# Second feed-forward product: weight sums by other formulas, one ahead of each of the third to sixth products

## The chip, the core and the metric

The kernel runs on one core of a Trainium2 chip. A core has a matrix engine (PE, with its weight loads listed apart as PEld), a vector engine (DVE), a scalar engine (ACT), a general engine (POOL) and a queue that issues transfers (SP). Each engine works through its own list of instructions; semaphores tie the lists together. PE sums its products in PSUM, a small memory of eight banks that DVE and ACT read out. The metric is device time in microseconds (us); before the change the median of three timed runs is 2292.98 us (2292.85 to 2294.41).

## The reference, cut to what matters

One transformer-like layer on 512 tokens of width 2048. Its last step, and the only one that the change touches, is the second product of the feed-forward part:

```python
D_MODEL = 2048
SEQ = 512
D_FF = -(-(8 * D_MODEL) // (3 * 256)) * 256      # 5632
...
h = rms_norm(x, norm2_g[layer]) * (1.0 + sc2) + sh2
gate, up = jnp.split(h @ w_ffn_in[layer], 2, axis=-1)
x = x + g2 * ((jax.nn.silu(gate) * up) @ w_ffn_out[layer])
```

All is float32. The second product is (512 x 5632) times (5632 x 2048).

## The kernel before, in words

**Seven products in place of eight.** The second product is done as a 2 x 2 block product by Winograd's form of Strassen's scheme: seven block products on sums and differences of the blocks. The weights' four blocks are called y[0] to y[3] in the code (y[0] top left, y[1] top right, y[2] bottom left, y[3] bottom right, each 128 partitions x n x 512 numbers). The sums of the other factor (the activations) are made ahead and lie in DRAM, from where `load_op` fetches them; the sums of the weights are made on DVE in this stage.

**Units.** The 44 row tiles of the inner dimension, paired by the scheme into 22, are cut into six chunks of 3, 3, 4, 4, 4 and 4 (`CHUNKS`), and the columns into two halves i. A pass over one chunk and one half is a unit; there are twelve, numbered u = 0 to 11. In a unit the seven products run in the order 2, 1, 7, 6, 4, 5, 3 (`ORDER`); the place of a product in that order is q = 0 to 6. Below, p2 is the product numbered 2, and so on.

**A product** (`multiply`, line 1195) goes through its chunk in pieces of two row tiles, here called halves h1 and h2 (in chunks of 3 the second half is one tile). Each half is first split into a high and a low part: ACT casts it to the matrix engine's reduced float (line 231), DVE subtracts the result from the original (line 232). PE then multiplies high by high, high by low and low by high, all into one bank: 12 matmuls of 128 x 512 per full half and pair of banks (j = 0 and 1), 24 for a product of four tiles. The halves' split tiles are named wfo in the profile (opsB for every fourth, which lies in spare room). In the engines' order below, wfo_2_0 is place q = 2 (p7), first half.

**The weight sums** of a unit are four, each on both halves. p2 and p1 take y[2] and y[0] as they are loaded and p3 takes y[3]; p7, p6, p4 and p5 take sums. Line 1268 makes y[0] = y[1] - y[0] ahead of p7; line 1202 makes y[1] = y[3] - y[1] for p7, t2 = y[3] - y[0] for p6 and y[2] = y[2] - t2 for p4. p5 takes the y[0] made ahead of p7. t2 is the tile T in the profile (from unit 1 on).

**Banks.** p1, p6, p5 and p3 write the two banks foA (foA_18351 is j = 0, foA_18352 is j = 1); p7 and p4 write foC; p2 writes foB. p1 starts foA anew, so its first matmul on a bank waits until p3's result of the unit before has been read out of it. That is the add `V.tensor_add(dst(0, j, 1), A[j], dst(0, j, 1))` at line 1289 (1285 after the change), on DVE, one for each bank. p1's own result is copied out by ACT (line 1222, in the first chunk line 1217).

**What sets the order.** The code is not run in the order written: a scheduler turns it into one fixed list for each engine, by dependencies and priorities. Splits and weight sums stand in `tc.high_priority(offset=AHEAD)` (300), ACT's copies out of foA and foC in twice that; the adds at line 1289 and 1282 have no raised priority.

**Loads.** y[0] and y[2] of the next unit are asked for at a unit's start, y[1] after p7 and y[3] after p3 (`load_y`, line 1048); y[1] and y[3] have one buffer each (yraw) that is loaded again when its last reader is done.

Of the kernel before, what the change touches and what calls it, by code (L numbers as in the profile page):

```python
# [26 lines left out]
CHUNKS = (3, 3, 4, 4, 4, 4)  # L27
ORDER = (2, 1, 7, 6, 4, 5, 3)
AHEAD = 300
# [100 lines left out]
def trunk(ctx, tc, a):  # L130
    nc = tc.nc
    V, S, G = nc.vector, nc.scalar, nc.gpsimd
# [91 lines left out]
    def split(r, shape, name):  # L224
        count[0] += 1
        if spare and count[0] % 4 == 0:
            hi, lo = spare[0](shape, name)
        else:
            hi, lo = ring_pair(shape, name)
        with tc.high_priority(offset=AHEAD):  # L230
            S.copy(hi, r)  # L231
            V.tensor_sub(lo, r, hi.bitcast(F32))  # L232
        return hi, lo
# [697 lines left out]
    for i, hs in enumerate(halves):  # L931
# [15 lines left out]
        y = rb[:, hs]  # L947
# [47 lines left out]
    for j in range(HALF):  # L995
        V.tensor_sub(block(0, 0, j), block(0, 1, j), block(0, 0, j))
        t2 = ft.tile([P, HT], F32, tag="t", name=f"t2_{j}")
# [35 lines left out]
    def place(n):  # L1033
        n %= 11
        return places[0][:, n] if n < 4 else places[1][:, n - 4] if n < 7 else places[2][:, n - 7]

    def load_op(c, q):
        if c < len(CHUNKS):
            nc.sync.dma_start(place(7 * c + q)[:, 0:CHUNKS[c]].bitcast(F32),
                              opd[c][:, ORDER[q] - 1].rearrange("p n (h t) -> p n h t", h=2))  # L1040

    def load_y(u, b):
        if u == len(units):
            return
        c, i = units[u]
        n = CHUNKS[c]
        t = raw_tile([P, n, T], f"wfo{u}_{b}") if b % 2 == 0 else yraw[u > 0][:, b // 2, 0:n]
        nc.sync.dma_start(t, a["w_fo"][i, b][:, starts[c]:starts[c] + n])
        blocks[u][b] = t
# [145 lines left out]
    def multiply(out, c, q, raw, first, u, sums):  # L1195
        n = CHUNKS[c]
        x = place(7 * c + q)
        for k0 in range(0, n, 2):
            w = min(2, n - k0)
            with tc.high_priority(offset=AHEAD):  # L1200
                for d, e, g in sums:
                    V.tensor_sub(*(t[:, k0:k0 + w] for t in (d, e, g)))
            whi, wlo = split(raw[:, k0:k0 + w], [P, w, T], f"wfo{u}_{q}_{k0}")
            for j in range(2):
                js = slice(j * P, j * P + P)
                for kk in range(w):
                    k = k0 + kk
                    flags = dict(stop=False, skip_group_check=True)
                    PE.matmul(out[j], x[:, k, 0, js], whi[:, kk], start=first and k == 0, **flags)
                    PE.matmul(out[j], x[:, k, 0, js], wlo[:, kk], start=False, **flags)  # L1210
                    flags["stop"] = k == n - 1
                    PE.matmul(out[j], x[:, k, 1, js], whi[:, kk], start=False, **flags)

    def onto(dst, src, first):
        if first:
            with tc.high_priority(offset=2 * AHEAD):
                S.copy(dst, src)
            return
        t = cond[:, taps[0] % 4 * T:taps[0] % 4 * T + T]
        taps[0] += 1  # L1220
        with tc.high_priority(offset=2 * AHEAD):
            S.copy(t, src)
        V.tensor_add(dst, dst, t)
# [14 lines left out]
    def some_out(n):  # L1238
        for _ in range(min(n, len(outs))):
            emit_out(*outs.pop(0))  # L1240

    for u, (c, i) in enumerate(units):
        def dst(th, j, dh):
            return O[:, 2 * th + j, dh * 1024 + i * T:dh * 1024 + i * T + T]

        def ready(th, dh):
            if c == last_c:
                outs.extend((8 * dh + 4 * i + m, th) for m in range(4))

        first, final = c == 0, c == last_c  # L1250
        if final and i == 0:
            for g in range(4):
                nc.sync.dma_start(place(7 * c + 7 + g).bitcast(F32).rearrange("p n h t -> p n (h t)"), x1d[:, 4 * g:4 * g + 4])
        if u == 2:
            nc.sync.dma_start(ident2, a["cst"][:, 0])
        y = blocks[u]
        t2 = (T2 if u else yraw[0][:, 2])[:, 0:CHUNKS[c]]
        load_y(u + 1, 2)
        load_y(u + 1, 0)
        for q, p in enumerate(ORDER):  # L1260
            out = {2: B[i], 7: C, 4: C}.get(p, A)
            raw = {2: y[2], 1: y[0], 7: y[1], 6: t2, 4: y[2], 5: y[0], 3: y[3]}[p]
            sums = {7: [(y[1], y[3], y[1])], 6: [(t2, y[3], y[0])], 4: [(y[2], y[2], t2)]}.get(p, ())
            if p == 7:
                with tc.high_priority(offset=AHEAD):
                    for k0 in range(0, CHUNKS[c], 2):
                        ks = slice(k0, min(k0 + 2, CHUNKS[c]))
                        V.tensor_sub(y[0][:, ks], y[1][:, ks], y[0][:, ks])
            multiply(out, c, q, raw, p in (1, 7) or p == 2 and first, u, sums)
            if final:  # L1270
                some_out(3)
            for j in range(2):
                if p == 1:
                    onto(dst(0, j, 0), A[j], first)
                    if final:
                        V.tensor_add(dst(0, j, 0), B[i][j], dst(0, j, 0))
                elif p == 7:
                    onto(dst(1, j, 1), C[j], first)
                elif p == 6:
                    onto(dst(1, j, 0), A[j], first)  # L1280
                elif p == 4:
                    V.tensor_add(dst(1, j, 0), C[j], dst(1, j, 0))
                elif p == 5:
                    onto(dst(1, j, 1), A[j], False)
                elif p == 3:
                    if first:
                        S.copy(dst(0, j, 1), A[j])
                    else:
                        V.tensor_add(dst(0, j, 1), A[j], dst(0, j, 1))
            if p == 1:  # L1290
                ready(0, 0)
                if final:
                    slots += [t[:, h * HT:h * HT + HT] for t in B[i] for h in range(2)]
            elif p in (4, 5, 3):
                ready(*{4: (1, 0), 5: (1, 1), 3: (0, 1)}[p])
            if p == 7:
                load_y(u + 1, 1)
            if p == 3:
                load_y(u + 1, 3)
            if u == 0 and q == 6:  # L1300
                places.append(hp.tile([P, 4, 4, 2, HT], F32R, tag="hhi", name="opsC"))
            if q < 4 and i == (c == 0):
                load_op(c + 1, q)
            if i == 1 and 1 <= q < 4:
                load_op(c + 1, q + 3)
# [60 lines left out]
```

## Time and profile before

| what | value |
|---|---|
| timed runs, median (lowest to highest) | 2292.98 us (2292.85 to 2294.41) |
| the profiled execution's own time | 2288.73 us |
| its span, first to last instruction | 2286.7 us |
| mean granted PE clock | 0.995 |
| PE busy over the span | 2228.2 us (97%) |
| DVE busy over the span | 1915.4 us (84%) |
| ACT busy over the span | 1156.0 us (51%) |
| second product, first and last matmul on foA, foB, foC start at | 1836.8 and 2278 us |

The profile is of one execution; its own time is 4.25 us under the median of the timed runs. In the rows of the timeline, the first number is the start in us from the span's start, the second the length; then engine, line, operation, output<-inputs, shape and count (xN merges N like instructions that follow each other). A bracket at the end says how long the engine was idle just before and which engine and line ended that.

### The profile page before, as it was taken

Reading aid. Unit: us, or ns where it says so; the run is one execution under the profiler, and the core shown is the slowest. Engines: PE = TensorE matmul, PEld = TensorE weight load, DVE = VectorE, ACT = ScalarE, POOL = GpSimd, SP = SyncE. Lnnn points to the kernel's source line nnn. Section 1 sums busy time; section 2 is a strip of 40 time slices with the busy share of each in tenths; the row PEclk is TensorE's granted clock in tenths of the full one; section 3 lists DMA queues with packets and bytes.
Section 4 is the critical chain, followed back from the end, with each engine's and each line's share of the span. In section 5 each row is a group of like instructions: output and inputs, shape, how many; then the busy total and the mean of one; then the engine's idle time right before and its main releaser. Section 6 shows DMA issues by size and latency. Waiting matters only on the chain.

```text
span 2286.7 us, 35537 instructions
## 1 busy us (share of the span) xinstructions
PE 2228.2 (97%) x14171; PEld 2025.8 (89%) x14171; DVE 1915.4 (84%) x2566; ACT 1156.0 (51%) x2015; POOL 10.0 (0%) x25
## 2 busy tenths in 40 slices
PE   7999899999999999999999999999999999999999
PEld 6899899878888878899999999999999977778787
DVE  8887779899887865599999888888888878888888
ACT  4326666566655522565454545455555445544443
POOL 0000000000000000000000000000000000000000
PEclk9999999999999999999999999999999999999999
DMA  9886546853332386346555644444444586666452
GB/s 369 314 326 220 174 145 228 303 188 111 112 110 74 111 310 228 97 143 226 185 208 198 225 149 169 150 153 166 132 171 143 178 310 225 238 221 221 151 199 75
DMA packets 114977, 437.68 MB, mean 191 GB/s; under 512 B 9822, under 2 KB 58236, under 8 KB 76796
## 3 DMA queue, kind: packets, MB, share of 16 engines
q1 hardware_dynamic: 114812, 435.42, 53.1%
q8 instruction: 111, 1.82, 0.3%
q14 instruction: 54, 0.44, 0.1%
HBM read 386.61 MB, written 48.77 MB: 190 GB/s over the span
## 4 chain that ended last, share of the span: by engine, by line
PE 64%; DVE 20%; DMA 7%; issue 5%; ACT 3%; SPq 0%; DVEq 0%; ACTq 0%
PE ffA L93 10%; PE foA L93 9%; PE wo L93 7%; PE sbp L93 7%; PE ffC L93 5%; PE foC L93 4%; PE st L93 4%; PE hgf L93 3%; PE hgg L93 3%; PE hgq L93 3%; DVE ff L232 3%; DMA opd<-fhi 2%; PE ffB L93 2%; PE ff L93 2%; DVE ada L179 1%
## 5 line engine op out<-in xcount | busy, mean ns | idle before, releaser
L93 PE MATMUL sbp<-wsb,hhi 128*128 128x384 f32 x1024 | 269.8, 343 | 3.1 <-DVE wsb L232 1.7
L179 DVE SCALAR_TENSOR_TENSOR ada<-ada,cond 128x2048 f32<-128x2048 f32 x95 | 217.0, 2289 | 48.1 <-DMA ada<-in_w_ada 47.9
L93 PEld LDWEIGHTS sbp<-wsb,hhi 128*128 128x128 f32 x1024 | 185.2, 190 | 7.9 <-issue 3.3
L93 PE MATMUL sbp<-wsb,hlo 128*128 128x384 f32 x512 | 172.9, 338 | 0.0
L93 PE MATMUL wo<-ohi,wo 128*128 128x512 f32 x480 | 150.2, 392 | 4.1 <-ACT wo L231 1.6
L232 DVE TENSOR_TENSOR wfo<-wfo,wfo 128x1024 fp32r<-128x1024 f32 (+1 forms) x72 | 83.3, 1164 | 39.7 <-ACT wfo L231 39.3
L93 PEld LDWEIGHTS wo<-ohi,wo 128*128 128x128 f32 x480 | 89.7, 188 | 24.3 <-ACT wo L231 2.9
L93 PE MATMUL ffA<-opD,ff 128*128 128x256 f32 x768 | 99.0, 286 | 4.0 <-ACT u L1027 4.0
L231 ACT CAST wfo<-wfo 128x1024 fp32r<-128x1024 f32 (+1 forms) x72 | 72.2, 1007 | 60.1 <-PE foA L93 56.9
L93 PE MATMUL ffC<-opC,ff 128*128 128x256 f32 x768 | 94.7, 279 | 5.8 <-ACT c L1027 5.8
L93 PEld LDWEIGHTS ffA<-opD,ff 128*128 128x128 f32 x768 | 95.6, 194 | 4.5 <-ACT u L1027 4.5
L1101 ACT CAST fhi<-forms 128x512 fp32r<-128x512 f32 (+1 forms) x63 | 43.7, 693 | 109.3 <-DMA opd<-fhi 76.2
L93 PEld LDWEIGHTS sbp<-wsb,hlo 128*128 128x128 f32 x512 | 97.0, 190 | 0.8 <-issue 0.5
L93 PEld LDWEIGHTS ffC<-opC,ff 128*128 128x128 f32 x768 | 90.8, 188 | 7.2 <-ACT c L1027 7.2
L93 PE MATMUL ffA<-opB,ff 128*128 128x256 f32 x768 | 93.3, 277 | 1.7 <-ACT ff L231 1.0
L93 PE MATMUL wo<-olo,wo 128*128 128x512 f32 x240 | 93.5, 390 | 0.1
L93 PE MATMUL ffB<-opA,ff 128*128 128x256 f32 x768 | 92.7, 276 | 0.0
L93 PEld LDWEIGHTS ffA<-opB,ff 128*128 128x128 f32 x768 | 90.1, 188 | 2.2 <-ACT ff L231 1.2
L93 PE MATMUL ffA<-opA,ff 128*128 128x256 f32 x744 | 89.9, 276 | 0.8 <-DVE ff L232 0.8
L93 PE MATMUL ffA<-opC,ff 128*128 128x256 f32 x744 | 90.1, 277 | 0.0
L93 PEld LDWEIGHTS ffB<-opA,ff 128*128 128x128 f32 x768 | 89.8, 188 | 0.0
L93 PE MATMUL ffC<-opB,ff 128*128 128x256 f32 x744 | 89.7, 276 | 0.0
(1008 smaller groups left out, 5955.5 us busy)
## 6 DMA issues: line engine op xcount, KB each, us to landing
ada<-in_w_ada SPq DMA_DIRECT2D x95, 1024.0 KB, 5.2
wfo<-in_w_fo SPq DMA_DIRECT2D x16, 1024.0 KB, 5.7
yraw<-in_w_fo SPq DMA_DIRECT2D x16, 1024.0 KB, 4.9
fix<-in_w_fix SPq DMA_DIRECT2D x14, 1024.0 KB, 5.5
opd<-forms SPq DMA_DIRECT2D x44, 256.0 KB, 4.7
opd<-fhi SPq DMA_DIRECT2D x42, 256.0 KB, 4.4
opsC<-opd SPq DMA_DIRECT2D x10, 1024.0 KB, 4.8
opsA<-opd SPq DMA_DIRECT2D x9, 1024.0 KB, 7.0
```

What stands on the lines that cost most here:

```text
L93: self.engine.matmul(out, lhsT, rhs, **kw)
L179: V.scalar_tensor_tensor(w, w, 1.0, row, op0=ALU.mult, op1=ALU.mult, accum_out=col)
L231: S.copy(hi, r)
L232: V.tensor_sub(lo, r, hi.bitcast(F32))
L1101: S.copy(hi, R[:, q])
```

## The change

t2 is the same quantity by another formula: y[3] - (y[1] - y[0]) becomes y[0] + (y[3] - y[1]), which uses the y[1] already made for p7. So the difference y[1] - y[0] isn't wanted before p6 any more. It is only p5's operand, and it is now made ahead of p5 as y[3] - t2. Each of p7, p6, p4 and p5 so has one sum made ahead of it; before, p7 had two and p5 none. Since y[1] is now read by p6's sum, its next load is asked for after p6 in place of p7. The numbers of sums, splits, matmuls and transfers stay the same.

```diff
             with tc.high_priority(offset=AHEAD):
-                for d, e, g in sums:
-                    V.tensor_sub(*(t[:, k0:k0 + w] for t in (d, e, g)))
+                for combine, *tiles in sums:
+                    combine(*(t[:, k0:k0 + w] for t in tiles))
...
-            sums = {7: [(y[1], y[3], y[1])], 6: [(t2, y[3], y[0])], 4: [(y[2], y[2], t2)]}.get(p, ())
-            if p == 7:
-                with tc.high_priority(offset=AHEAD):
-                    for k0 in range(0, CHUNKS[c], 2):
-                        ks = slice(k0, min(k0 + 2, CHUNKS[c]))
-                        V.tensor_sub(y[0][:, ks], y[1][:, ks], y[0][:, ks])
+            sums = {7: [(V.tensor_sub, y[1], y[3], y[1])], 6: [(V.tensor_add, t2, y[0], y[1])],
+                    4: [(V.tensor_sub, y[2], y[2], t2)], 5: [(V.tensor_sub, y[0], y[3], t2)]}.get(p, ())
             multiply(out, c, q, raw, p in (1, 7) or p == 2 and first, u, sums)
...
-            if p == 7:
+            if p == 6:
                 load_y(u + 1, 1)
```

The scheduler's lists change with it, at three places that the prediction speaks of.

**DVE in unit 8**, from the split of p1's first half on. L232 is a split's subtraction, L1202 and L1268 are the sums, L1289 and L1285 the adds that read p3's result of the unit before out of foA. First before, then after:

```order
L232 TENSOR_TENSOR wfo_1_0_20166<-wfo_0_19890,wfo_1_0_20166 128x1024
L1289 TENSOR_TENSOR O<-foA_18351,O 128x512
L1268 TENSOR_TENSOR wfo_0_19890<-yraw,wfo_0_19890 128x1024
L232 TENSOR_TENSOR wfo_1_2_20181<-wfo_0_19890,wfo_1_2_20181 128x1024
L1202 TENSOR_TENSOR yraw<-yraw 128x1024
L1268 TENSOR_TENSOR wfo_0_19890<-yraw,wfo_0_19890 128x1024
L1202 TENSOR_TENSOR T_18348<-yraw,wfo_0_19890 128x1024
L232 TENSOR_TENSOR wfo_2_0_20204<-yraw,wfo_2_0_20204 128x1024
L1202 TENSOR_TENSOR yraw<-yraw 128x1024
L1202 TENSOR_TENSOR T_18348<-yraw,wfo_0_19890 128x1024
```

```order
L1202 TENSOR_TENSOR yraw<-yraw 128x1024 x2
L232 TENSOR_TENSOR wfo_1_2_20181<-wfo_0_19890,wfo_1_2_20181 128x1024
L1202 TENSOR_TENSOR T_18348<-wfo_0_19890,yraw 128x1024
L232 TENSOR_TENSOR wfo_2_0_20202<-yraw,wfo_2_0_20202 128x1024
L1202 TENSOR_TENSOR T_18348<-wfo_0_19890,yraw 128x1024
L1202 TENSOR_TENSOR wfo_2_19888<-wfo_2_19888,T_18348 128x1024
L232 TENSOR_TENSOR opsB<-yraw,opsB 128x1024
L1202 TENSOR_TENSOR wfo_2_19888<-wfo_2_19888,T_18348 128x1024
L232 TENSOR_TENSOR wfo_3_0_20238<-T_18348,wfo_3_0_20238 128x1024
L1202 TENSOR_TENSOR wfo_0_19890<-yraw,T_18348 128x1024 x2
L1285 TENSOR_TENSOR O<-foA_18351,O 128x512
```

Before, the add for the first bank stood right behind the split of p1's first half, and the one for the second bank (not shown) after all eight sums. Now both stand after all eight sums, the first one thirteen instructions behind that split, the second two rows further. Units 6 and 10 read the same. In units 5, 7 and 9 the new list reads, behind the split of p2's second half: sum y[1] h1, split p1 h1, sum y[1] h2, sum t2 h1, split p1 h2, sum t2 h2, split p7 h1, sum y[2] h1 and h2, split p7 h2, sum y[0] h1, split p6 h1, sum y[0] h2, and then the two adds.

**PE in unit 8**, from the last matmuls of p2 on, before and after:

```order
L93 MATMUL foB_18354<-opsB 128x512 x6
L93 MATMUL foA_18351<-wfo_1_0_20166,opsC 128x512 x6
L93 MATMUL foA_18351<-wfo_1_2_20181,opsC 128x512 x6
L93 MATMUL foC<-wfo_2_0_20204,opsC 128x512 x12
L93 MATMUL foC<-opsB,opsC 128x512 x12
L93 MATMUL foA_18351<-wfo_3_0_20241,opsC 128x512 x2
L93 MATMUL foA_18352<-wfo_1_0_20166,opsC 128x512 x6
L93 MATMUL foA_18352<-wfo_1_2_20181,opsC 128x512 x6
```

```order
L93 MATMUL foB_18354<-opsB 128x512 x6
L93 MATMUL foC<-wfo_2_0_20202,opsC 128x512 x12
L93 MATMUL foC<-opsB,opsC 128x512 x12
L93 MATMUL foA_18351<-wfo_1_0_20166,opsC 128x512 x6
L93 MATMUL foA_18351<-wfo_1_2_20181,opsC 128x512 x2
L93 MATMUL foA_18352<-wfo_1_0_20166,opsC 128x512 x6
L93 MATMUL foA_18351<-wfo_1_2_20181,opsC 128x512 x4
L93 MATMUL foA_18352<-wfo_1_2_20181,opsC 128x512 x6
```

Before, p1's twelve matmuls on the first bank stood between p2 and p7. Now p7 follows p2 at once, and all of p1 comes behind it. This is so in unit 3 and in units 5 to 11; unit 4 keeps p1's first bank ahead of p7.

**DVE at the end of unit 0**, as the difference of the two lists; T and yraw are here those of unit 1, wfo_5_0 and wfo_5_2 the splits of p5 in unit 0:

```order
 L1102 TENSOR_TENSOR forms_18089<-forms_18089,cond 128x768
-L232 TENSOR_TENSOR wfo_5_0_18496<-wfo_0_18314,wfo_5_0_18496 128x1024
+L1202 TENSOR_TENSOR yraw<-yraw 128x1024
+L1202 TENSOR_TENSOR yraw<-yraw 128x512
+L1202 TENSOR_TENSOR T_18348<-wfo_0_18360,yraw 128x1024
+L1202 TENSOR_TENSOR T_18348<-wfo_0_18360,yraw 128x512
+L232 TENSOR_TENSOR wfo_5_0_18495<-wfo_0_18314,wfo_5_0_18495 128x1024
 L232 TENSOR_TENSOR wfo_5_2_18511<-wfo_0_18314,wfo_5_2_18511 128x512
```

The first four sums of unit 1 now stand ahead of the split of p5 in unit 0.

## The prediction

> **What bounds the kernel now.** I read the page's engine rows first, then busy time by stretches for two units in the middle of the second product, then PE's own timeline for the stretches in which it is idle, with what ended each.
>
> ```profile
> PE 2228.2 (97%) x14171; PEld 2025.8 (89%) x14171; DVE 1915.4 (84%) x2566; ACT 1156.0 (51%) x2015; POOL 10.0 (0%) x25
> ...
> 2114.00:2153.00 39.00, 38.47 (x169) 31.38 (x168) 33.18 (x35) 18.72 (x22) 0.00 (x0) 1.00 0.49 176
> 2153.00:2192.00 39.00, 38.47 (x169) 31.23 (x168) 33.17 (x35) 18.71 (x22) 0.00 (x0) 1.00 0.63 227
> ...
> 1852.98 5.97 PE L93 MATMUL foA<-wfo,opsA 128*128 128x512 f32 x18 [3.71 <-ACT O L1217]
> ...
> 1935.00 0.50 PE L93 MATMUL foC<-wfo,opsC 128*128 128x512 f32 x1 [0.26 <-ACT wfo L231]
> 1936.66 3.92 PE L93 MATMUL foC<-wfo,opsC 128*128 128x512 f32 x16 [1.16 <-DVE wfo L232]
> 1969.18 2.83 PE L93 MATMUL foC<-wfo,opsB 128*128 128x512 f32 x11 [1.28 <-DVE wfo L232]
> 2011.34 2.83 PE L93 MATMUL foC<-wfo,opsB 128*128 128x512 f32 x11 [0.53 <-DVE wfo L232]
> ...
> 2206.86 2.79 PE L93 MATMUL foC<-opsB 128*128 128x512 f32 x11 [0.53 <-DVE opsB L232]
> ```
>
> PE is the bound: in a unit of 39 us it is busy for 38.47 at full granted clock (1.00), DVE for 33.2. What PE loses is small and sits at one spot: in units 3 to 10 it stops in p7 (the bank foC) for a split that DVE finishes late, 0.53 each in units 5 to 10. In unit 0 it waits 3.71 for ACT's copies. So time can change only where DVE makes PE wait. The rows of unit 8 show how the queues meet:
>
> ```profile
> 2114.43 1.05 ACT L231 CAST wfo<-wfo 128x1024 fp32r<-128x1024 f32 x1 [1.19 <-PE foA L93]
> 2115.52 1.23 DVE L232 TENSOR_TENSOR wfo<-wfo,wfo 128x1024 fp32r<-128x1024 f32 x1 [1.02 <-ACT wfo L231]
> 2116.66 0.69 DVE L1289 TENSOR_TENSOR O<-foA,O 128x512 f32<-128x512 f32 x1
> 2116.95 2.88 PE L93 MATMUL foB<-wfo,opsB 128*128 128x512 f32 x12
> 2117.26 1.22 DVE L1268 TENSOR_TENSOR wfo<-yraw,wfo 128x1024 f32<-128x1024 f32 x1
> 2118.40 1.22 DVE L232 TENSOR_TENSOR wfo<-wfo,wfo 128x1024 fp32r<-128x1024 f32 x1
> 2119.53 1.22 DVE L1202 TENSOR_TENSOR yraw<-yraw 128x1024 f32<-128x1024 f32 x1
> 2120.92 1.06 ACT L231 CAST wfo<-yraw 128x1024 fp32r<-128x1024 f32 x1 [2.71 <-DVE yraw L1202]
> 2122.39 2.88 PE L93 MATMUL foA<-wfo,opsC 128*128 128x512 f32 x12
> 2125.11 2.88 PE L93 MATMUL foC<-wfo,opsC 128*128 128x512 f32 x12
> 2127.48 1.22 DVE L232 TENSOR_TENSOR opsB<-yraw,opsB 128x1024 fp32r<-128x1024 f32 x1
> 2128.75 2.79 PE L93 MATMUL foC<-opsB,opsC 128*128 128x512 f32 x11 [0.53 <-DVE opsB L232]
> 2130.88 0.69 DVE L1289 TENSOR_TENSOR O<-foA,O 128x512 f32<-128x512 f32 x1
> ```
>
> Three durations come from here. DVE starts a full half (128x1024) every 1.14 (2117.26, 2118.40, 2119.53). A matmul takes 0.2267: the 24 of p2 run from 2116.95 to 2122.39. PE goes on 1.27 to 1.29 after the start of the split that it waits for (2127.48 to 2128.75), which is 0.05 to 0.07 after that split's 1.22; an add of 0.69 should so free its bank 0.76 after its start. The stall of 0.53 costs 0.69 of PE's pace: by 0.2267 the 14th matmul of p7 was due at 2125.11 + 13 x 0.2267 = 2128.06 and came at 2128.75.
>
> **The change part by part.** The sums stay eight halves a unit. The rows show 1.22 for every full half, at lines 232, 1202 and 1268, all subtractions; no row has an add of that size, and I take 1.22 for it too (a half size add at line 1289 takes 0.69, which leaves no room for a much slower one). So DVE's busy time stays, and only places matter.
>
> *The gain.* In unit 8 the two halves of line 1268 leave the stretch ahead of p7's second split, 2.28 us. Taken alone that ends the 0.69 there.
>
> *The loss in units 6, 8 and 10.* Line 1289's add for the first bank goes from right behind the split of p1's first half to behind all eight sums, and p1 goes behind p7 on PE. I lay the new DVE list of unit 8 at 1.14 a step from the split at 2115.52, which doesn't move: its cast waited for PE (1.19 <-PE foA). Sum y[1] 2116.66 and 2117.80, split p1 h2 2118.94, t2 h1 2120.08, split p7 h1 2121.22, t2 h2 2122.36, y[2] h1 2123.50, split p7 h2 2124.64, y[2] h2 2125.78, split p6 h1 2126.92, y[0] 2128.06 and 2129.20, add of the first bank 2130.34, bank free 2131.10. ACT's casts are in time: the one for p7 h1 had been free for 2.71 when DVE's sum let it go at 2120.92, and that sum is now earlier. PE: p2 ends at 2122.39, p7 follows; its second half starts 2125.11, its second matmul, the first that reads the split, is due at 2125.34 and gets it at 2124.64 + 1.29 = 2125.93, 0.59 late. p7 ends 11 matmuls on, at 2128.42, and p1 then waits for the bank until 2131.10: 2.68. Together 3.27, against 0.69 before: 2.58 lost. The same from another side: when the add's bank comes free, PE has 48 matmuls of the unit done; before, at that time, it had about 60, for p1's first twelve had filled the stretch. Twelve are 2.72.
>
> *The loss in units 5, 7 and 9.* Rows of unit 9:
>
> ```profile
> 2147.72 0.33 SPq L1048 DMA_DIRECT2D yraw<-in_w_fo  x1
> 2152.28 1.22 DVE L232 TENSOR_TENSOR wfo<-wfo,wfo 128x1024 fp32r<-128x1024 f32 x1 [0.26 <-ACT wfo L231]
> 2155.95 5.60 PE L93 MATMUL foB<-wfo,opsB 128*128 128x512 f32 x24
> 2164.11 3.11 PE L93 MATMUL foC<-wfo,opsC 128*128 128x512 f32 x13
> 2167.76 2.79 PE L93 MATMUL foC<-wfo,opsC 128*128 128x512 f32 x11 [0.53 <-DVE wfo L232]
> ...
> DMA to landing us min/median/max: 4.7/4.9/6.6
> ```
>
> From the split of p2's second half at 2152.28 the list given with the change runs: y[1] h1 2153.42, split p1 h1 2154.56, y[1] h2 2155.70, t2 h1 2156.84, split p1 h2 2157.98, t2 h2 2159.12, split p7 h1 2160.26, y[2] 2161.40 and 2162.54, split p7 h2 2163.68, y[0] h1 2164.82, split p6 h1 2165.96, y[0] h2 2167.10, first add 2168.24, bank free 2169.00. PE: p2 ends 2161.39, p7's first half 2164.11; the split is there at 2164.97, due 2164.34: 0.63. p7 ends 2167.46, p1 waits until 2169.00: 1.54. Together 2.17 against 0.70 (2167.76 less 2164.11 + 13 x 0.2267): 1.47 lost. The new first step needs y[3], whose load is issued at 2147.72; by the median landing, 4.9, it is there at 2152.6, by the longest, 6.6, at 2154.3, 0.9 late, which would hold everything behind it on DVE.
>
> Three units of either kind: 3 x 2.58 + 3 x 1.47 = 12.15.
>
> The trace shows the order being kept: the second bank's add at 2130.88 ran 14 us after p3's last matmul (before 2116.95), behind other work whose place was ahead of it. The Trainium skill, page "PSUM — Partial Sum Buffer", section "Engine vs sequencer instructions", has ScalarE's and VectorE's queues as strictly first in, first out, and matmuls as starting in program order; by that rule the waits above stand in full, and without it, DVE taking the add when its input is ready and PE passing over p1, the sum would be that of the first rival below.
>
> *Unit 0.* The split of p5's first half now stands behind four sums of unit 1, and these need unit 1's y[3]:
>
> ```profile
> 1855.72 1.83 SPq L1048 DMA_DIRECT2D yraw<-in_w_fo  x1
> 1858.71 1.23 DVE L232 TENSOR_TENSOR wfo<-wfo,wfo 128x1024 fp32r<-128x1024 f32 x1 [5.06 <-ACT wfo L231]
> 1862.86 4.24 PE L93 MATMUL foA<-wfo,opsB 128*128 128x512 f32 x18
> ...
> yraw<-in_w_fo SPq DMA_DIRECT2D x1, 768.0 KB, 6.0
> ```
>
> Issued at 1855.72 it lands 6.0 later, at 1861.72. Then 1.14 + 0.60 + 1.14 + 0.60 (a short half takes just over half a long one) = 3.48: the split starts at 1865.20 in place of 1858.71 and serves PE at 1866.49; p5 wants it from its second matmul, 1863.09. 3.4 lost; by landings of 4.7 and 6.6 from the row above, 2.1 to 4.0. The 3.71 ahead of p6 stays: the DVE work that ACT's copies hang on is the same amount.
>
> *Units 1 to 4.* PE has no idle row in units 1 and 2 today, and their p1 waits for ACT's copies of p3 (line 1287), not for an add. In 3 and 4 the second add still stands behind the eighth sum, so an earlier p7 only brings PE sooner to that bank. I take 0, between the end of both stalls, -(0.26 + 1.16 + 1.28) = -2.7, and twice 1.47.
>
> *Unit 11.* It has unit 9's list, but transposes of finished outputs stand between its matmuls and fill a part: 0.7, the middle of 0 and 1.47.
>
> *y[1]'s load* goes out after p6's sum and behind one more transfer on SP's queue. It is next read some 25 us later and lands in 4.9 (longest 6.6): 0. Without that cover it would cost a landing a unit.
>
> Sum: 12.15 + 3.4 + 0 + 0.7 = 16.2. On the span of 2286.7 this gives 2302.9, on the profiled execution's 2288.73 it gives 2304.9; the timed median lies 4.25 above that execution, so **2309 us**, 0.7% slower.
>
> **The rivals.**
>
> *Faster: the adds hold nobody.* If a free bank or other ready work carries PE past p1's wait, only the gain is left. For it: today PE never waits for line 1289 in these units. Against: that is so because the add stood early. It pays 6 x 0.69 + 2.7 = 6.8: 2286. It decides if the add is done by the end of p7, which needs 2.7 less of DVE work ahead of it in unit 8 and 1.5 in unit 9; the y[0] sums behind the adds (2.28) would nearly do.
>
> *No change: the stall only changes its name.* DVE does as much before the second bank's add as before, so PE may find its lost twelve matmuls elsewhere in the unit, as later slack on DVE (5.8 us of 39 a unit). Then -4 in p7 and +4 in p1, 2293, and with unit 0 alone 2296. Against: PE is in order and busy 38.47 of 39; a stall of it has no slack to be made up from.
>
> *Worse: y[3]'s load also holds DVE.* At the longest landing, 0.9 in each of units 5, 7 and 9, with the high ends of units 3 and 4 and of unit 0: 2309 + 2.7 + 2.9 + 0.6 = 2315.
>
> **How the numbers follow.** Forecast 0.75, worse 0.06 (together slower), a loss under half of the sum, still over 0.2%, 0.03; no change 0.10; faster 0.06. About 0.2%, 4.6 us, is what a measurement of this kernel can tell from none. The forecast's own range is 2303 (unit 0 at 2.1, units 3 and 4 gaining 2, unit 11 at 0, and a quarter microsecond less in each of six units) to 2315; to hold 8 in 10 I go down to 2299, toward the smaller loss. Slower 0.84, same 0.10, faster 0.06.
>
> **What would show it.** PE's timeline should show, in units 5 to 10, a short stop in foC and a longer one at foA, released by DVE O L1285: some 1.3 in odd units and 2.5 in even ones; the unit pair takes about 82 us in place of 78. In unit 0, a stop of about 3 at p5's foA, released by DVE wfo L232. DVE's busy time stays at 1915. The forecast is wrong if no stop at foA names L1285, or if p7's stop is gone and nothing came for it.

## The result, and the profile after

The changed kernel takes **2310.26 us** (median of five runs, 2308.31 to 2311.66) against 2292.85 for the kernel before in the same session (five runs, 2289.72 to 2294.41): a ratio of 1.0076, 95% interval 1.0064 to 1.0087. It is 17.4 us slower; 16.2 were forecast.

The engines' rows of the page after, and busy time in the stretches of units 8 and 9:

```profile
PE 2236.8 (97%) x14171; PEld 2028.4 (88%) x14171; DVE 1915.9 (83%) x2566; ACT 1156.6 (50%) x2015; POOL 10.0 (0%) x25
...
2131.00:2172.00 41.00, 38.28 (x168) 30.97 (x167) 33.81 (x35) 18.79 (x22) 0.00 (x0) 1.00 0.38 129
2172.00:2213.00 41.00, 39.38 (x172) 31.58 (x171) 32.70 (x35) 18.96 (x23) 0.00 (x0) 1.00 0.70 255
```

DVE is busy for 1915.9 in place of 1915.4: the sums cost what they did, the addition included. PE's matmuls are as many, and two units now fill 82 us where two took 78 before. Nothing got more to do; things wait more. The chronological rows of unit 8 show where:

```profile
2130.62 1.22 DVE L232 TENSOR_TENSOR wfo<-wfo,wfo 128x1024 fp32r<-128x1024 f32 x1 [1.01 <-ACT wfo L231]
2131.76 2.35 DVE L1202 TENSOR_TENSOR yraw<-yraw 128x1024 f32<-128x1024 f32 x2
2132.05 2.88 PE L93 MATMUL foB<-wfo,opsB 128*128 128x512 f32 x12
...
2139.71 1.22 DVE L232 TENSOR_TENSOR opsB<-yraw,opsB 128x1024 fp32r<-128x1024 f32 x1
...
2140.98 2.79 PE L93 MATMUL foC<-opsB,opsC 128*128 128x512 f32 x11 [0.36 <-DVE opsB L232]
2141.98 1.22 DVE L232 TENSOR_TENSOR wfo<-T,wfo 128x1024 fp32r<-128x1024 f32 x1
2143.11 2.35 DVE L1202 TENSOR_TENSOR wfo<-yraw,T 128x1024 f32<-128x1024 f32 x2
2145.39 0.68 DVE L1285 TENSOR_TENSOR O<-foA,O 128x512 f32<-128x512 f32 x1
2146.12 11.22 PE L93 MATMUL foA<-wfo,opsC 128*128 128x512 f32 x48 [2.36 <-DVE O L1285]
```

The split of p1's first half starts at 2130.62; the add that frees p1's bank starts at 2145.39, 14.8 later, where it was 1.1 before (2115.52 to 2116.66). p7's second half waits 0.36 for its split, ends, and p1 then stands 2.36 for the add. Unit 9 has the same two stops, the second one shorter:

```profile
2182.46 2.79 PE L93 MATMUL foC<-wfo,opsC 128*128 128x512 f32 x11 [0.39 <-DVE wfo L232]
2183.46 1.22 DVE L232 TENSOR_TENSOR wfo<-T,wfo 128x1024 fp32r<-128x1024 f32 x1
2184.59 1.22 DVE L1202 TENSOR_TENSOR wfo<-yraw,T 128x1024 f32<-128x1024 f32 x1
2185.73 1.28 DVE L1285 TENSOR_TENSOR O<-foA,O 128x512 f32<-128x512 f32 x2
2186.47 3.01 PE L93 MATMUL foA<-wfo,opsC 128*128 128x512 f32 x12 [1.22 <-DVE O L1285]
```

The waits of the second product after the change, summed (what waits, for what, us in all, how often, the longest), have a name that they did not have before (six of the seven are the stops of units 5 to 10, the seventh is one of 0.30 in unit 4):

```profile
PE foA L93 <- DVE O L1285: 11.0, 7, 2.4
```

Unit 0 has a stop of its own. The rows are the weight loads of p6 and p5 and DVE's work between, and p5's matmuls behind the stop; the last two give the granted clock (the number behind POOL's) of two stretches:

```profile
1857.96 5.54 PEld L93 LDWEIGHTS foA<-wfo,opsA 128*128 128x128 f32 x18 [4.05 <-ACT O L1217]
1866.40 1.83 DVE L1202 TENSOR_TENSOR yraw<-yraw 128x1024 f32<-128x1024 f32 x2 [7.78 <-DMA yraw<-in_w_fo]
1868.15 1.82 DVE L1202 TENSOR_TENSOR T<-wfo,yraw 128x1024 f32<-128x1024 f32 x2
1869.89 1.82 DVE L232 TENSOR_TENSOR wfo<-wfo,wfo 128x1024 fp32r<-128x1024 f32 x2
1871.16 5.33 PEld L93 LDWEIGHTS foA<-wfo,opsB 128*128 128x128 f32 x17 [3.35 <-DVE wfo L232]
1871.16 5.76 PE L93 MATMUL foA<-wfo,opsB 128*128 128x512 f32 x17 [2.93 <-DVE wfo L232]
...
1864.00:1871.00 7.00, 4.23 (x19) 3.18 (x17) 4.60 (x5) 3.14 (x5) 0.00 (x0) 1.00 0.48 191
1871.00:1877.00 6.00, 5.84 (x18) 4.54 (x19) 3.99 (x7) 1.43 (x3) 0.00 (x0) 0.72 0.67 224
```

DVE stands 7.78 for unit 1's y[3], then makes four half sums of unit 1, and only then the split that unit 0's p5 wants. PE's weight loads pause 3.35. The 17 loads that follow take 5.33, and the granted clock is 0.72 in that stretch. In the same place before, 18 loads took 4.04, without a pause:

```profile
1862.64 4.04 PEld L93 LDWEIGHTS foA<-wfo,opsB 128*128 128x128 f32 x18
```

Where the time went by units, from the starts of p2 in both traces (the last one from the span's end):

| unit | lost, us | forecast |
|---|---|---|
| 0 | 4.75 | 3.4 |
| 1 to 4 together | 0.1 | 0 |
| 5, 7, 9 | 1.40, 1.42, 1.47 | 1.47 each |
| 6, 8, 10 | 2.37, 2.45, 2.44 | 2.58 each |
| 11 | 1.74 | 0.7 |
| sum | 18.1 | 16.2 |

The spans differ by 23.2 (2309.9 and 2286.7). The other 5.1 lie ahead of the stage: its first matmul starts at 1841.90 in place of 1836.84, behind instructions that are the same in both kernels. In the thirteen profiles of this study that start lies anywhere from 1833.4 to 1843.9. So the tables below also give the **stage time**, from that first matmul to the span's end: 449.9 before, 468.0 after.

### The profile page after: what moved, and what is told of

Its sections match the earlier page's. It is cut to its first block, busy times and chain, and to the rows that moved or that the text cites. A ratio compares the mean times of both kernels' runs of the same rounds, so it can differ in the third digit from the quotient of the medians.

```text
span 2309.9 us, 35503 instructions
## 1 busy us (share of the span) xinstructions
PE 2236.8 (97%) x14171; PEld 2028.4 (88%) x14171; DVE 1915.9 (83%) x2566; ACT 1156.6 (50%) x2015; POOL 10.0 (0%) x25
## 4 chain that ended last, share of the span: by engine, by line
PE 61%; DVE 21%; DMA 9%; issue 5%; ACT 3%; SPq 0%; DVEq 0%; ACTq 0%
PE ffA L93 9%; PE foA L93 8%; PE sbp L93 8%; PE wo L93 7%; PE ffC L93 4%; PE st L93 4%; PE hgf L93 4%; PE hgg L93 3%; PE hgq L93 3%; DMA opd<-fhi 3%; PE foC L93 3%; DVE ff L232 3%; PE ffB L93 2%; DVE wfo L232 2%; DVE wfo L1202 2%
## 5 line engine op out<-in xcount | busy, mean ns | idle before, releaser
L179 DVE SCALAR_TENSOR_TENSOR ada<-ada,cond 128x2048 f32<-128x2048 f32 x95 | 216.7, 2286 | 39.5 <-DMA ada<-in_w_ada 39.2
L232 DVE TENSOR_TENSOR wfo<-wfo,wfo 128x1024 fp32r<-128x1024 f32 (+1 forms) x72 | 83.5, 1163 | 38.3 <-ACT wfo L231 38.2
```

The source lines that it names most:

```text
L179: V.scalar_tensor_tensor(w, w, 1.0, row, op0=ALU.mult, op1=ALU.mult, accum_out=col)
```

## The experiments

Each ratio is to the kernel before in the same session. Its median was 2291.30 to 2293.40 in the four sessions, so times of different sessions compare only to within some 2 us.

**1. The adds early.** The two adds of line 1285 get raised priority, once in the changed kernel and once in the kernel before:

```diff
                     else:
-                        V.tensor_add(dst(0, j, 1), A[j], dst(0, j, 1))
+                        with tc.high_priority(offset=2 * AHEAD):
+                            V.tensor_add(dst(0, j, 1), A[j], dst(0, j, 1))
```

> The changed kernel with one thing added: the two adds of p3 that read foA out (line 1285) get the raised priority that ACT's copies have. Theory (p1 waits because these adds stand behind the eight weight sums): the stops at foA released by DVE O L1285 go, and since p1 then runs ahead of p7 the short stops in foC go too. A pair of units took 82.0 after the change; 168 matmuls at 0.2267 are 38.1, so a pair without stops is some 76.8 with the 0.3 a unit that are lost without any stop: 3 x 5.2 = 15.6 less than the changed kernel's 2310.3, and up to 5 more for the stops in units 3, 4 and 11: 2290 to 2295. Rival (the stall only changes its name, as DVE has as much to do before p1 as ever): within 3 of 2310. Rival (half is the formulas themselves): 2300 to 2305.

> Control: the kernel before, with the same raised priority on its adds (line 1289). If the adds' place is what the change spoilt, they held nobody before, and there is only the late split of p7 to win: 0.69 in six units and 2.7 in units 3 and 4, 6.8 at most: 2286 to 2293. If the raised priority gains by itself, whatever the formulas, the gain here is as large as in the changed kernel: 15 or more, below 2279.

Measured, with raised adds: the changed kernel 2284.97, ratio to the kernel before 0.9965 (0.9952 to 0.9978), stage 444.6; the kernel before 2281.00, ratio 0.9947 (0.9934 to 0.9960), stage 440.1. PE's rows of unit 8 in the changed kernel with raised adds, with DVE's first add (now line 1286), and the stretch of units 7 and 8:

```profile
2116.96 1.28 DVE L1286 TENSOR_TENSOR O<-foA,O 128x512 f32<-128x512 f32 x2
...
2117.25 2.88 PE L93 MATMUL foB<-wfo,opsB 128*128 128x512 f32 x12
2119.97 2.88 PE L93 MATMUL foB<-opsB 128*128 128x512 f32 x12
2122.69 5.60 PE L93 MATMUL foA<-wfo,opsC 128*128 128x512 f32 x24
2128.13 2.88 PE L93 MATMUL foC<-wfo,opsC 128*128 128x512 f32 x12
...
2079.17:2155.33 76.16, 76.16 (x338) 63.08 (x336) 66.11 (x69) 37.87 (x44) 0.00 (x0) 1.00 0.58 207
```

No row of units 1 to 10 carries a stop: p1 follows p2, p7 follows p1, and PE is busy for all of 76.16. The rivals fall: the stall did not change its name (2284.97, not 2310), and the formulas are not the cost. The size was beyond the forecast range of 2290 to 2295: the stage gained 23.4, where 20.6 was the most forecast. Some 2 of the difference are the 0.3 a unit that the forecast took as lost without any stop. 2 x 168 matmuls at 0.2267 are 76.2, and the pair takes exactly that. So the 0.3 were stops as well. In the kernel before, the weight loads of unit 9 show them, too short for a row of PE, with the stretch of its units 7 and 8:

```profile
2174.44 1.24 PEld L93 LDWEIGHTS foA<-wfo,opsC 128*128 128x128 f32 x6 [0.19 <-ACT cond L1222]
2176.79 2.14 PEld L93 LDWEIGHTS foA<-opsB,opsC 128*128 128x128 f32 x10 [0.19 <-DVE opsB L232]
...
2077.78:2155.95 78.17, 77.11 (x337) 62.67 (x336) 66.44 (x69) 37.44 (x44) 0.00 (x0) 1.00 0.56 202
```

This is part of why the control gained more than the 6.8 forecast at most: 12.4 by the medians, 9.8 by the stage times. Units 5 to 10 gained 6.0 where 4.1 was forecast, units 3 and 4 gained 3.75 where 2.7 was; the other 2.6 of the medians lie outside the stage. The control's gain is some 13 us smaller than the changed kernel's 25. What the change spoilt is the adds' place; what the control gained was there to be had before.

**2. Unit 0 alone.** Unit 1's sums for p7 and p6 are queued behind unit 0's last split on DVE (`made0` holds that split's instruction; only the order is set, nothing waits for the split to finish):

```diff
+                with behind(made0[0] if u == 1 and ORDER[q] in (7, 6) else None):
                     for combine, *tiles in sums:
                         combine(*(t[:, k0:k0 + w] for t in tiles))
```

> The changed kernel with unit 1's sums for p7 and p6 put behind unit 0's last split on DVE, nothing else. Theory: the stop ahead of p5 in unit 0 (2.93 idle, and 17 matmuls that then took 5.33 in place of 3.85, at a granted clock of 0.72) goes as a whole: 4.7 less, 2305.6. If only the stop goes and the slow matmuls come from something else: 3.2 less, 2307. If the wait for y[3]'s load only moves to unit 1: 2310.

Measured: 2304.96, ratio 1.0057 (1.0043 to 1.0072), stage 463.9. Against 2310.26 that is 5.3 less, though the interval overlaps that of the change (1.0064 to 1.0087); the stage is 4.1 shorter. The stops at foA in units 5 to 10 are as after the change (1.22 and 2.35). p5's stop is gone and so are its slow matmuls:

```profile
1854.64 6.75 PEld L93 LDWEIGHTS foA<-wfo,opsA 128*128 128x128 f32 x18 [4.04 <-ACT O L1225]
1865.51 4.04 PEld L93 LDWEIGHTS foA<-wfo,opsB 128*128 128x128 f32 x18
```

The second row is p5, at full pace. The first is p6 behind its old stop, and here it took 6.75 in place of 5.54. Those 1.2 of the stage don't come from the edit: with the same edit p6 took 5.57 in one later profile and 6.64 in another, and without it 6.66 in a third. Unit 0 takes 31.2 in place of 34.9 after the change; with the 1.2 counted in, that is the whole loss of 4.75, slow matmuls included, as the theory had it.

**3. Is it y[0]'s later place?** The new formulas, with y[0]'s sum moved from p5 to right behind t2:

```diff
-            sums = {7: [(V.tensor_sub, y[1], y[3], y[1])], 6: [(V.tensor_add, t2, y[0], y[1])],
-                    4: [(V.tensor_sub, y[2], y[2], t2)], 5: [(V.tensor_sub, y[0], y[3], t2)]}.get(p, ())
+            sums = {7: [(V.tensor_sub, y[1], y[3], y[1])], 6: [(V.tensor_add, t2, y[0], y[1]), (V.tensor_sub, y[0], y[3], t2)],
+                    4: [(V.tensor_sub, y[2], y[2], t2)]}.get(p, ())
```

> The changed kernel's formulas, but y[0] = y[3] - t2 is made right behind t2, ahead of p6, in place of ahead of p5. Theory (any sums that are ready at raised priority stand ahead of the adds, wherever among them y[0]'s is): no change, 2308 to 2312. Rival (moving y[0]'s sum back to p5 is what pushed the adds back): some 2 x 1.14 in each of six units less, about 2297.

Measured: 2308.16, ratio 1.0068 (1.0054 to 1.0081), stage 468.4: no change beyond the intervals. Unit 8 reads as after the change:

```profile
2144.88 11.17 PE L93 MATMUL foA<-wfo,opsC 128*128 128x512 f32 x48 [2.35 <-DVE O L1285]
```

Where among the sums y[0] is made does not matter, as long as all of them go ahead of the add.

**4. The sums that do stand ahead of the adds, moved behind them.** Only y[0]'s two half sums are queued behind the second add of the unit before (`adds` lists these adds so far):

```diff
+                with behind(adds[-1] if ORDER[q] == 5 and adds else None):
                     for combine, *tiles in sums:
                         combine(*(t[:, k0:k0 + w] for t in tiles))
```

> The changed kernel with only y[0]'s two half sums put behind the previous unit's second add on DVE. The adds come free 2 x 1.14 = 2.28 earlier. Theory: the stops of 1.22 at foA in units 5, 7 and 9 go and those of 2.35 shrink to 0.1 to 0.4, so 10 to 16 less: 2294 to 2300; a stop in foC stays. Rival (something else ahead of the adds holds them too): less than 5.

Measured: 2293.74, ratio 1.0004 (0.9995 to 1.0014), stage 450.6: 16.5 less than after the change, just past the larger end. In unit 8 (the adds are line 1291 here) the first add now starts while p7's second half is running, and the scheduler puts p1 into the middle of p7:

```profile
2133.56 0.39 PE L93 MATMUL foC<-opsB,opsC 128*128 128x512 f32 x1
...
2134.18 0.69 DVE L1291 TENSOR_TENSOR O<-foA,O 128x512 f32<-128x512 f32 x1
2134.32 0.97 PE L93 MATMUL foC<-opsB,opsC 128*128 128x512 f32 x3 [0.38 <-DVE opsB L232]
2135.13 5.62 PE L93 MATMUL foA<-wfo,opsC 128*128 128x512 f32 x24
```

The stop at foA is gone, the one in foC stays, as forecast. So taking 2.28 us of sums out of the adds' way is enough. That the time is again that of the kernel before is a sum of two parts: unit 0 keeps its stop at p5 (3.56 by the weight loads) and takes 35.1 in place of 30.1, while units 3 to 10 together take 4.5 less than before the change.

**5. The bank freed by ACT.** ACT copies p3's two banks out at raised priority, and DVE adds the copies later; DVE's sums and adds keep their late places:

```diff
                     else:
-                        V.tensor_add(dst(0, j, 1), A[j], dst(0, j, 1))
+                        onto(dst(0, j, 1), A[j], False)
```

> The changed kernel, but ACT copies p3's banks out first, as it does for p1 and p6, and DVE adds the copy later. DVE's order of sums stays and its adds stay late, but the bank no longer waits for them; ACT gets two more copies a unit of some 0.55 each. Theory (it is the bank that p1 waits for, not DVE's work as such): as with raised adds, 2284 to 2289. Rival (DVE is too late with p7's and p1's splits anyway): above 2300.

Measured: 2286.30, ratio 0.9976 (0.9968 to 0.9985), stage 445.3, with no stop in units 1 to 10. p1 waited for the bank, not for DVE as such: in unit 8 DVE still makes all eight sums ahead of its adds.

**6. Why the adds fell back.** Before, p7's first sum wrote y[0], so it had to come behind p1's splits, which read y[0]. The new formula has no such tie. Here it is put back, with nothing said of the adds: y[1]'s first half behind p1's first split, the second behind p1's second (`made` lists the splits so far, and `made[-2]` is that split in both cases):

```diff
+                with behind(made[-2] if ORDER[q] == 7 and u else None):
                     for combine, *tiles in sums:
                         combine(*(t[:, k0:k0 + w] for t in tiles))
```

> The changed kernel with the y[1] sums for p7 put behind the splits of p1 on DVE, from unit 1 on; nothing is said of the adds. Theory (before, p7's first sum overwrote y[0], so it had to come behind p1's splits, and that left the adds their early place; the new formula has no such tie, so the sums run up and the adds fall behind): the adds go back ahead of most sums, the stops at foA released by L1285 go, and the time falls by 12 to 18, to 2292 to 2298. Rival (the adds are late for their low priority alone, whatever the sums are tied to): 2308 to 2312.

Measured: 2292.43, ratio 1.0002 (0.9994 to 1.0011), stage 450.8. The first add is early again, and p1 again runs ahead of p7:

```profile
2117.04 0.68 DVE L1291 TENSOR_TENSOR O<-foA,O 128x512 f32<-128x512 f32 x1
2118.92 2.88 PE L93 MATMUL foB<-opsB 128*128 128x512 f32 x12
2121.64 2.88 PE L93 MATMUL foA<-wfo,opsC 128*128 128x512 f32 x12
2124.36 2.88 PE L93 MATMUL foC<-wfo,opsC 128*128 128x512 f32 x12
```

The same holds in units 5 to 10, which take 38.6 to 38.8 each (unit 10 40.9) where 39.0 to 39.2 (41.2) was the time before the change. Unit 0's stop at p5 is gone as well, since unit 1's sums now come behind unit 0's splits too. In unit 11 the tie isn't enough: both adds again stand behind all eight sums there, p1 behind p7, and PE stops for an operand of p4; the unit takes 53.8 in place of the 50.5 before:

```profile
2248.37 0.50 PE L93 MATMUL foC<-wfo,opsB 128*128 128x512 f32 x1 [2.11 <-ACT wfo L233]
```

So the total equals that of the kernel before, but the units do not. That low priority alone made the adds late is refuted for units 5 to 10: the priority was the same in all three kernels. What else decides the adds' place in unit 11 stays open.

**7. Both cures.** Raised adds and unit 1's sums later, in the changed kernel; and, since medians and stage times did not agree there on what unit 0's part is worth, the three best kernels once more, in one session:

> Both cures in the changed kernel: raised priority for p3's adds and unit 1's sums behind unit 0's last split. If the two losses are apart, they add: 2285.0 (raised adds alone) less 4.7 to 5.3 (unit 0's part) gives 2280, the same as the kernel before with raised adds (2281.0). If they overlap, it stays at 2283 to 2285.

> The changed kernel with raised adds once more, now on the same chip as the two that follow, since the stage's own time (5.5 us apart in the traces) and the timed ratios (0.9965 and 0.9963) disagree on whether unit 0's loss adds to the other. Theory: 5 more than with both cures. Rival: no difference, unit 0's stop being made up elsewhere ahead of or behind the stage.

> Both cures. Theory: 5 less than with raised adds alone, and within 1 of the kernel before with raised adds (stage times 439.1 and 440.1). Rival: as raised adds alone.

> The kernel before with raised adds: 10 to 12 less than the kernel before, as the first time (0.9947), and within 1 of both cures in the changed kernel, so that with the adds early and unit 1's sums out of the way the two sets of formulas cost the same.

| kernel | first: us, ratio (interval), stage | again: us, ratio (interval), stage |
|---|---|---|
| changed, adds early | 2284.97, 0.9965 (0.9952 to 0.9978), 444.6 | 2283.34, 0.9969 (0.9958 to 0.9981), 443.1 |
| changed, both cures | 2282.33, 0.9963 (0.9951 to 0.9975), 439.1 | 2280.86, 0.9951 (0.9939 to 0.9964), 440.3 |
| before, adds early | 2281.00, 0.9947 (0.9934 to 0.9960), 440.1 | 2279.96, 0.9952 (0.9938 to 0.9966), 439.8 |

Changed with both cures, and before with the adds early, end in the same stage time, 439 to 440: the formulas cost the same once the orders are mended. Both are 0.4 to 0.5% faster than the kernel before. (In the first column, the row with both cures is of another session than the other two.) Unit 0's part measured 5.5 of the stage the first time and 2.8 the second: p5's stop was 3.96 with slow matmuls behind it in the one profile, 2.84 with none in the other. The timed medians give 2.6 and 2.5, with intervals that overlap: that the two losses add is shown by the stage times, and the timing alone doesn't settle it.

## Why the prediction was right, and where not

**The mechanism held, step by step.** p1 behind p7 on PE, the adds behind eight sums on DVE, and PE with no other work at that point: stops of 1.22 and 2.36 at foA, released by L1285, short stops in foC that stayed (0.36 to 0.39). Counted by PE's pace of 0.2267 a matmul, the stops at foA are 1.52 in unit 9 and 2.65 in unit 8, where 1.54 and 2.68 were worked out, and those in foC 0.57 and 0.52, where 0.63 and 0.59 were. The six units lost 11.55 of the 12.15 forecast. The trace agrees with the rule of strict order in VectorE's queue (the Trainium skill, page "PSUM — Partial Sum Buffer", section "Engine vs sequencer instructions"): in unit 8 the add's input had been ready since p3 ended, before 2132.05, and the add started at 2145.39, behind the last sum.

**The add's cost, the load, units 1 to 4.** Taking 1.22 for the addition was right: 19 of them average 1.218, the 19 subtractions in the same place before 1.222. No row shows DVE waiting for y[1]'s later load, and units 1 to 4 lost 0.1 together.

**Unit 0, 3.4, was mis-sized.** The stop came as worked out (2.93 by PE's rows, 3.35 by the weight loads'), but the sum ended there. After the stop PE ran at a granted clock of 0.72, and its 17 matmuls took 1.7 longer than at full pace (5.59 from the first's start to p2's, at 0.2267 they take 3.85): 4.75 in all. The sum priced a stop by its length alone, though the trace of before had shown the same at p6: the 18 matmuls of "1852.98 5.97", behind a stop of 3.71, are 1.73 longer than the 4.24 of p5's 18.

**Unit 11, 0.7, was mis-sized.** It lost 1.74, more than an ordinary odd unit (1.40 to 1.47). The transposes of finished outputs, which were to fill a part of the stop, wait themselves for DVE's output operation (line 1234), and that stands behind the same sums:

```profile
2265.69 2.36 DVE L1202 TENSOR_TENSOR wfo<-yraw,T 128x1024 f32<-128x1024 f32 x2
2267.97 1.22 DVE L232 TENSOR_TENSOR wfo<-T,wfo 128x1024 fp32r<-128x1024 f32 x1
2269.10 0.87 DVE L1234 SCALAR_TENSOR_TENSOR O<-foB,mod,opsC 128x256 f32<-128x256 f32 x2
2269.63 0.83 PE L98 MATMUL foB<-ident,O 128*128 128x128 f32 x4 [0.63 <-DVE O L1234]
```

**The rivals.** "The adds hold nobody" needed the banks free by p7's end, or nearly; experiments 1, 4 and 5 do this in three ways, and each takes 16 to 25 us off. "The stall only changes its name" would have kept them near 2310. "y[3]'s load also holds DVE" did not happen in units 5, 7 and 9. It did once outside unit 0, in unit 2, where DVE stood 2.23 for it; PE's following p7 took 0.38 longer, which is the 0.4 that unit 2 lost:

```profile
1910.58 1.83 DVE L1202 TENSOR_TENSOR yraw<-yraw 128x1024 f32<-128x1024 f32 x2 [2.23 <-DMA yraw<-in_w_fo]
...
1917.74 3.26 PE L93 MATMUL foC<-wfo,opsC 128*128 128x512 f32 x12
```

**Luck in the last microsecond.** The stage lost 18.1, 1.9 more than the sum: unit 0 and unit 11 were 2.4 too small together, and the six units 0.6 too large. The medians lie 17.4 apart, and the one measured is 1.3 from the 2309 forecast. That it is so near is partly luck, since the stretch ahead of the stage isn't steady: the profiled execution lay 4.25 below its runs' median before the change and 1.40 above it after, with the stage starting 5.1 later, and no reading of this stage could have told.

## What to carry to other kernels

When a change frees an instruction from an order that it only had by accident (here a sum that overwrote an operand still being read), ask what low-priority work lived in the gap that this order left: a read-out of a PSUM bank that falls back by a few instructions is a stop of the matrix engine. Such read-outs should have at least the priority of the work that prepares the next operands; that one line gave 0.5% on the kernel before. And price a stop of PE not by its length alone, once it nears the length behind which the trace shows a lower granted clock.

## What the runs showed of the hardware

Stops of PE in unit 0 let the granted clock fall, not always, and for a varying time. The rows give pauses of the weight loads and the time of the loads behind them; at full pace 18 take 4.04. First two of the kernel in experiment 5 (granted clock 1.00 in the time of the first, 0.57 in that of the second), then one of the second run of the raised adds (1.00):

```profile
1855.10 3.98 PEld L93 LDWEIGHTS foA<-wfo,opsA 128*128 128x128 f32 x18 [4.05 <-ACT O L1217]
...
1868.41 6.20 PEld L93 LDWEIGHTS foA<-wfo,opsB 128*128 128x128 f32 x17 [5.03 <-DVE wfo L232]
```

```profile
1868.31 3.74 PEld L93 LDWEIGHTS foA<-wfo,opsB 128*128 128x128 f32 x17 [2.84 <-DVE wfo L232]
```

Pauses of 2.84 and of 2.77 (units 6, 8 and 10) never slowed the loads behind them. Of thirteen pauses of 4.04 to 4.13 ahead of p6, twelve did, by 1.4 to 2.7, and one, the first row above, did not at all. The five of 3.35 to 5.03 ahead of p5 all did: 17 loads took 5.33 or 5.34 in four, 6.20 behind the longest. The bound so lies between 2.84 and 3.35 here. The Trainium skill, page "TensorE: Matmul & The Clock Gate", section "What's actually happening", has the clock halved behind an idle window of about 3.4 us that runs free of the kernel, and restored behind a busy one as long. The trace agrees with the length, nearly, but the free-running window doesn't account for the counts: as an estimate from the page's 3.4, such a window lies whole within a pause of 4.05 in about 0.65/3.4, one case in five, and never within one of 3.35, and here twelve of thirteen and that one slowed PE. Why the one pause of 4.05 cost nothing stays open. No run here varied the pause by itself.
